# Rebuilding the opening of a hybrid attention layer: modulation sums on TensorE, rotation tables inside attention

## The chip, the cores and the metric

The kernel runs on one core of one Trainium2 chip. A core has five engines with an instruction stream each: TensorE (PE in the profile; its weight loads are PEld), VectorE (DVE), ScalarE (ACT), GpSimd (POOL) and SyncE (SP), which here issues nearly all transfers. An engine takes its instructions in the order in which they stand; engines wait for each other by semaphores. The metric is the device time of one execution in microseconds (us), as the median of several runs.

## The reference

One layer of an encoder: 1024 tokens of width 1024, all in float32. A conditioning vector `c` gives six vectors that shift, scale and gate; the change touches how the first two, shift and scale of the first norm, are computed.

```
mod = silu(c) @ w_ada + b_ada            # 6 x 1024
sh_a, sc_a, g_a, sh_m, sc_m, g_m = split(mod, 6)
h = rmsnorm(x, g_attn_norm) * (1 + sc_a) + sh_a
q_lat, kv_lat, k_rope, ca_qkv = split(h @ w_in)
q = rmsnorm(rmsnorm(q_lat) @ w_q_up)     # 8 heads of 64 + 32
k, v from rmsnorm(kv_lat) @ w_kv_up, k_rope
q, k = rope on the last 32 columns (positions up to some thousands)
o_mla = chunk-causal attention(q, k, v)  # 8 latent heads
o_ca = attention over a 9-chunk band with relative bias  # 8 band heads
x = x + g_a * (concat(o_mla, o_ca) @ w_out)
h = rmsnorm(x, g_mlp_norm) * (1 + sc_m) + sh_m
u = causal_depthwise_conv3(h @ w_up); gate, val = split(u)
x = x + g_m * ((silu(gate) * val) @ w_down)
```

## The kernel before

**Precision and stages.** Products keep float32 quality by splitting each operand into a high and a low part (`hi_of`, L77 to L80, and `lo_of`, L83) and adding three products (`gemm3`, L172 to L174). The kernel is one pass: an opening stage, attention with the other projections as filler, the output projection, the MLP. Its text is sorted by a list scheduler when the program is built: each instruction goes to its engine's list in an order that follows readiness and priority, and not just the text. `tc.issue_after(x)` adds an edge: what is written inside stands behind instruction `x`. `tc.high_priority` moves attention's own steps ahead of filler.

**Opening stage.** SP loads the packed parameters, the eight tiles of `x`, `c` spread over all partitions, then per column block `d` (128 columns, eight of them) two tiles of modulation weights of 512 KB (`load_ada`, L230, tag `wa`, five buffers) and the first query-key weights (`load_w`, L206, raw tiles in three buffers). Each `x` tile gets its sum of squares on ScalarE (L285), its power on GpSimd (L123, L124) and its factor on VectorE (L287). For block `d` VectorE computes shift and scale by two reductions over 1024 products (L389) and one product (L390) into `modT`; `mod_transpose` lets TensorE turn four blocks of `x` (L364), ScalarE applies scale and shift (L369, L370), GpSimd or VectorE make the low part; then 24 products per block add to the first query-key projection in four banks of PSUM (`qk0`).

**Rotation tables.** `rope_tables` reduces position times frequency to an angle in a chain of small VectorE steps on 128x128 elements (L302, L303, L308, L335, L338, L343, L345, L346), takes two Sins on ScalarE (L344, L347) and multiplies gains into two tables (L353). The latent group's `f_m` and `f_up` read these tables much later.

**Tables of ScalarE.** Silu, Sin, Ln and Exp are looked up in a set of functions that has to be loaded. The build puts a load in front of an activation whose function is not in the set loaded at that place of the list; `act.preload_act_table_set(name)` is a load of a set chosen by name. The kernel has one, behind the second Sin:

```
with tc.issue_after(last_trig[0].ins):
    act.preload_act_table_set("natural_log_exp_and_others")
```

**Attention.** 32 units follow each other: 16 of the band heads, 16 of the latent heads, two query halves per head. A unit runs `guard` (a row minimum per query, L796 to L812), `mrow` (L820, L821), then per key block `st` (scores L858, Exp L862, second Exp L866 or a copy on GpSimd, low part on VectorE L869) and two blocks later `val` (L884 to L886) into one accumulator of PSUM with one buffer. After a unit's last block, Ln and Exp form the reciprocal (L891, L892) and VectorE multiplies it in (L893). Filler generators, called by `pace` on a budget of estimated TensorE time, run the other projections: values `f_v`, query-key `f_qk`, latent `f_m`, `f_up`, and `f_oca`; their normalisations use `rsqrt_att`, an Ln and an Exp per call (L137, L138) between VectorE steps. `f_ada` (L515, L520) computes the other modulation vectors on the side. Before the first unit, filler is run up to a budget of `W_IN / 2`, half of the first value projection.

Of the kernel before, what the change touches and what calls it, by code (L numbers as in the profile page):

```python
# [23 lines left out]
P = 128  # L24
# [8 lines left out]
BIG16 = 60000.0  # L33
BSC = 256.0
# [30 lines left out]
def layer_kernel(ctx, tc, I, out):  # L65
# [78 lines left out]
    hw = right.__enter__()  # L144
    att_pg = tc.tile_pool(name="apg", bufs=1, side="left")
# [6 lines left out]
    ps = psA.__enter__()  # L152
    startp = tc.tile_pool(name="start", bufs=1, side="left")
# [37 lines left out]

    def load_w(name, src, ncol, he="a", ssw=None):
        tiles = []
        for k in range(ND):
            if ncol <= 256:
                w = hw.tile([P, 2, 256], F32R, name=f"{name}s{k}", tag="ws", bufs=16)
                hi, lo = w[:, 0, :ncol], w[:, 1, :ncol]
            else:
                wh = hw.tile([P, 512], F32R, name=f"{name}h{k}", tag="ws", bufs=16)
                wl = hw.tile([P, 512], F32R, name=f"{name}l{k}", tag="ws", bufs=16)  # L200
                hi, lo = wh[:, :ncol], wl[:, :ncol]
            for c0 in range(0, ncol, 256):
                c = slice(c0, min(c0 + 256, ncol))
                raw = hw.tile([P, 256], F32, name=f"{name}r{k}_{c0}", tag="wr", bufs=3)
                rw = raw[:, :c.stop - c0]
                sp.dma_start(rw, src[:, k, c])  # L206
                if ssw is not None:
                    junk = qtile(f"{name}j{k}")
                    act.activation(junk[:, :c.stop - c0], rw, AF.Square, accum_out=ssw[:, k:k + 1])
                hi_of(he, hi[:, c], rw)  # L210
                lo_of("p", lo[:, c], rw, hi[:, c])
            tiles.append((hi, lo))
        return tiles
# [7 lines left out]
    for t in range(NT):  # L221
        xt = pgtile([P, D], F32, f"x{t}") if t < 4 else st.tile([P, D], F32, name=f"x{t}", tag="x", bufs=4)
        sp.dma_start(xt[:], I["x"][t * P:(t + 1) * P, :])
        xs.append(xt)
# [7 lines left out]

    csb = st.tile([P, D], F32, name="csb")
# [47 lines left out]
    load_ada(0)  # L281
# [8 lines left out]
    last_trig = []  # L290

    def rope_tables():
        buf = [st.tile([P, 4, NT, 16], F32, name=f"rt{i}") for i in range(6)]
        cnt = [-1]

        def T():
            cnt[0] += 1
            return buf[cnt[0] // 4 % 6][:, cnt[0] % 4]

        def rnd(src, q):  # L300
            o = T()
            dve.tensor_scalar(o, src, q, MAGIC, op0=MUL, op1=ADD)  # L302
            dve.tensor_scalar(o, o, MAGIC, None, op0=SUB)  # L303
            return o

        def fma(n, c, b):
            o = T()
            dve.scalar_tensor_tensor(o, n, c, b, op0=MUL, op1=ADD)  # L308
            return o

        p1 = _grid(TWO_PI, 2.0 ** -9)
        p2 = _grid(TWO_PI - p1, 2.0 ** -21)
        p3 = TWO_PI - p1 - p2

        def reduce(src):
            n = rnd(src, 1.0 / TWO_PI)
            r = fma(n, -p1, src)
            r = fma(n, -p2, r)
            return fma(n, -p3, r)
# [6 lines left out]
        nh = rnd(ang, 2.0 ** -20)  # L326
        rem = fma(nh, -(2.0 ** 20), ang)
        nm = rnd(rem, 2.0 ** -8)
        lo = fma(nm, -(2.0 ** 8), rem)
        tot = reduce(lo)  # L330
        for n, w in ((nh, 2.0 ** 20), (nm, 2.0 ** 8)):
            c = w - round(w / TWO_PI) * TWO_PI
            c1 = _grid(c, 2.0 ** -9)
            x = T()
            dve.tensor_scalar(x, n, c1, None, op0=MUL)  # L335
            x = fma(n, c - c1, reduce(x))
            y = T()
            dve.tensor_tensor(y, tot, x, op=ADD)  # L338
            tot = y
        tot = reduce(tot)  # L340
        pi_s = 3.1415925
        sn, cn, cl, c2, cl2 = T(), T(), T(), T(), T()
        dve.tensor_scalar(cl, tot, pi_s, -pi_s, op0=MIN, op1=MAX)  # L343
        act.activation(sn, cl, AF.Sin)  # L344
        dve.tensor_scalar(c2, tot, math.pi / 2, None, op0=ADD)  # L345
        dve.tensor_scalar(cl2, reduce(c2), pi_s, -pi_s, op0=MIN, op1=MAX)  # L346
        last_trig.append(act.activation(cn, cl2, AF.Sin))  # L347

        for tab, c0 in ((tabq, C_RQ), (tabk, C_RK)):
            for half, trig in ((0, cn), (1, sn)):  # L350
                for j in range(2):
                    o = half * 32 + j * 16
                    dve.tensor_tensor(tab[:, :, o:o + 16], trig,  # L353
                                      pk[:, c0 + j * 16:c0 + j * 16 + 16].unsqueeze(1)
                                      .to_broadcast([P, NT, 16]), op=MUL)

    rope_tables()


    def mod_transpose(src, k, h, row, pspool, psum_tag, pb, hpool, tag, tmp, nbuf, heng, leng):  # L360

        pt = pspool.tile([P, 512], F32, name=f"ht_ps{row}_{k}_{h}", tag=psum_tag, bufs=pb)
        for j in range(4):
            pe.transpose(pt[:, j * P:(j + 1) * P], src(j), ident[:])  # L364
# [5 lines left out]
        act.activation(v[:], pt[:], AF.Identity, scale=a, bias=b)  # L370
# [7 lines left out]
    wqk = load_w("wq0_", I["w_qk"][0], 256)  # L378
    qk0s = ps.tile([P, 1024], F32, name="qk0_s", tag="S", bufs=1)
    qk0t = [ps.tile([P, 512], F32, name=f"qk0_{i}", tag="ST", bufs=2) for i in range(2)]  # L380
    qk0 = [qk0s[:, :512], qk0s[:, 512:], qk0t[0][:], qk0t[1][:]]
    for d in range(ND):
        if d + 1 < ND:
            load_ada(d + 1)

        tmp = cst.tile([P, 1], F32, name=f"adat{d}", tag="adat", bufs=2)
        for i, (init, o) in enumerate(((bsc[:, d:d + 1], tmp[:]), (pk[:, C_B + d:C_B + d + 1], modT[:, 1, d:d + 1]))):
            w = wada[2 * d + i]
            dve.tensor_tensor_reduce(w[:], w[:], csb[:], 1.0, init, MUL, ADD, accum_out=o)  # L389
        dve.tensor_tensor(modT[:, 0, d:d + 1], tmp[:], pk[:, C_GA + d:C_GA + d + 1], op=MUL)  # L390
# [10 lines left out]
    with tc.issue_after(last_trig[0].ins):  # L401
        act.preload_act_table_set("natural_log_exp_and_others")
# [67 lines left out]
    def v_tiles(pl, name, n):  # L470
        vs = [pl.tile([P, 4, 2, 3, 64], F16, name=f"{name}{i}") for i in range(n)]
        for v in vs:
            dve.memset(v[:, :, 0, 1], 1.0)
            dve.memset(v[:, :, 1, 1], 0.0)
        return vs
# [9 lines left out]
    def f_v(pp):  # L485
        ssw = cst.tile([P, ND], F32, name=f"ssw{pp}")
        w = load_w(f"wv{pp}_", I["w_v"][pp], 256, ssw=ssw)
# [20 lines left out]
    def f_ada():  # L508
        for m in (2, 3, 4):
            for n in range(4):  # L510
                acc = atile(f"aacc{m}_{n}")
                c0 = m * D + n * 256
                for k in range(ND):
                    w = atile(f"aw{m}_{n}_{k}")
                    sp.dma_start(w[:], I["w_ada"][k * P:(k + 1) * P, c0:c0 + 256])  # L515
                    if k == 0:
                        with tc.issue_after(last_lo["v"].ins):
                            dve.tensor_scalar(acc[:], w[:], cs[:, 0:1], None, op0=MUL)
                    else:
                        dve.scalar_tensor_tensor(acc[:], w[:], cs[:, k:k + 1], acc[:], op0=MUL, op1=ADD)  # L520
# [49 lines left out]
    def f_m():  # L570
        w = load_w("wm_", I["w_m"], NM)
# [42 lines left out]
    def f_up_steps(gr):  # L614
        if gr == 0:
            right.__exit__(None, None, None)
# [106 lines left out]
    ident_h = at.tile([P, P], F16, name="ident_h")  # L723
    dve.tensor_copy(ident_h[:], ident[:])
    ident_b = at.tile([P, P], F16, name="ident_b")
    dve.tensor_scalar(ident_b[:], ident[:], BSC, None, op0=MUL)
    mk_q = at.tile([P, P], F16, name="mk_q")
    mk_k = at.tile([P, P], F16, name="mk_k")
    for m_ in (mk_q, mk_k):
        pool.memset(m_[:], 0.0)  # L730
    pool.memset(mk_q[0:1, 0:64], BIG16)
    pool.memset(mk_q[32:33, 64:128], BIG16)
    pool.memset(mk_k[32:33, 0:64], BIG16)
    mz = at.tile([P, QK + 4], F16, name="mz")
    for x in kts:
        dve.memset(x[64:65, 1], 1.0)
    dve.memset(mz[:], 0.0)

# [26 lines left out]
    class Unit:  # L765
# [58 lines left out]
        def st(u, x):  # L824
# [7 lines left out]
            with tc.high_priority(offset=OFF_S):  # L832
# [29 lines left out]
                act.activation(p[:, :w], s[:, :w], AF.Exp, scale=ninv)  # L862
# [6 lines left out]
                dve.tensor_tensor(hl[:, 1, :w], p[:, :w], hl[:, 0, :w], op=SUB)  # L869
# [74 lines left out]
    fillers = [("v0", f_v(0)), ("qk1", f_qk(1)), ("qk2", f_qk(2)), ("v1", f_v(1)), ("qk3", f_qk(3)),  # L944
# [5 lines left out]
    ca_done = []  # L950
    ga_done = []
# [31 lines left out]
    knots = [(0.0, W_IN / 2), (14 * C_CA, W_A), (16 * C_CA + 6 * C_M, W_A + W_UP + O_EARLY * W_O),  # L983
# [19 lines left out]
    def value():  # L1003
# [3 lines left out]
        return u.val(x)  # L1007

    while spent[0] < W_IN / 2:
# [375 lines left out]
def _inputs(a):  # L1385
# [34 lines left out]
    wa_a = np.stack([wa[:, D:2 * D], wa[:, :D]], 1).reshape(D, 2, ND, P).transpose(2, 1, 3, 0)  # L1420
    d = {
# [31 lines left out]
```

## Time and profile before

| what | value |
|---|---|
| median of 3 runs | 1436.58 us (1432.51 to 1441.64) |
| profiled execution, its own time | 1435.16 us |
| its span, first to last instruction | 1433.2 us |
| mean granted TensorE clock | 0.960 |
| first softmax (L862) starts | 108.3 us |
| last unit's Ln (L891) starts | 684.4 us |
| MLP's first Silu (L1251) | 791.4 us |

A row of the table of stretches gives, for a stretch of the span, the busy time and the number of instructions of each engine, the granted TensorE clock (1.00 is full speed), the mean busy share of the DMA engines and the GB/s moved. A row of instruction groups gives line, engine, operation, output and input tiles, count, busy time and mean ns of one, then the idle time ahead of them with what ended it. A row of a line's or a tile's answer gives minimum, median and maximum of the duration in ns, and the first and last start in us. A row of the timeline gives start, duration, engine, line, operation and, in brackets, the idle time before it and the releaser.

### The profile page before, as it was taken

What the parts mean: (1) busy time and instruction counts of PE and PEld (TensorE: products, weight loads), DVE (VectorE), ACT (ScalarE), POOL (GpSimd) and SP (SyncE); (2) the same over time, 40 slices, a digit from 0 to 9 for tenths busy, and PEclk for the clock granted to TensorE, in tenths of its full rate; (3) what the DMA queues carried; (4) which work ended last, traced back from release to release, by engine and by line L of the source; (5) the groups of instructions that cost most, each with busy time, mean ns of one, the idle gap of its engine ahead of it and who ended that gap; (6) DMA issues with size and microseconds to landing.
All of it is one profiled execution on the core that took longest, in us unless ns stands there. A gap on an engine that the chain in (4) does not pass through costs nothing.

```text
span 1433.2 us, 20250 instructions
## 1 busy us (share of the span) xinstructions
PE 1286.3 (90%) x6952; PEld 868.0 (61%) x6952; DVE 1071.7 (75%) x1721; ACT 806.8 (56%) x1517; POOL 728.2 (51%) x776
## 2 busy tenths in 40 slices
PE   3869999988867889898897999999999988999998
PEld 3758878866544556555663444444444437888887
DVE  8865775666789887876467999988888876666554
ACT  5446675555766766665476566666666533333331
POOL 5643234342345362524350787666666626666664
PEclk9979999999978999999998999999999998999999
DMA  8321223221110033332813632222221005446542
GB/s 313 118 92 38 82 73 109 87 74 45 56 41 22 16 103 99 105 100 84 315 61 117 212 104 89 88 89 89 88 89 59 30 30 206 146 141 225 181 152 103
DMA packets 83458, 153.03 MB, mean 107 GB/s; under 512 B 8598, under 2 KB 44698, under 8 KB 83356
## 3 DMA queue, kind: packets, MB, share of 16 engines
q1 hardware_dynamic: 83356, 151.75, 31.5%
q8 instruction: 54, 0.88, 0.2%
q14 instruction: 48, 0.39, 0.1%
HBM read 122.88 MB, written 28.84 MB: 106 GB/s over the span
## 4 chain that ended last, share of the span: by engine, by line
PE 59%; DVE 19%; DMA 9%; ACT 5%; issue 4%; POOL 2%; SPq 0%; DVEq 0%; ACTq 0%; POOLq 0%
PE p L1127 7%; PE p L1126 7%; PE p L1128 7%; DMA aw<-w_ada 6%; PE dn L1368 6%; PE dn L1369 6%; PE dn L1370 5%; PE tm L858 2%; DVE adaw L389 2%; DVE aacc L520 2%; PE tc L858 2%; DVE mz L812 1%; DVE hlm L869 1%; PE ipq L172 1%; PE ipq L174 1%
## 5 line engine op out<-in xcount | busy, mean ns | idle before, releaser
L83 POOL TENSOR_TENSOR wds<-wd,wds 128x512 fp32r<-128x512 f32 x88 | 152.1, 1748 | 105.1 <-ACT wds L77 105.1
L1368 PE MATMUL dn<-wds,g 128*128 128x512 f32 x352 | 136.8, 395 | 9.1 <-ACT g L77 9.1
L77 ACT ACTIVATE wds<-wd 128x512 fp32r<-128x512 f32 x88 | 54.7, 623 | 153.1 <-PE dn L1370 148.3
L1369 PE MATMUL dn<-wds,g 128*128 128x512 f32 x352 | 137.1, 392 | 0.0
L1370 PE MATMUL dn<-wds,g 128*128 128x512 f32 x352 | 135.6, 390 | 0.0
L1355 DVE TENSOR_TENSOR wd<-wd,gmbc 128x1024 f32<-128x1024 f32 x44 | 72.6, 1654 | 83.6 <-DMA wd<-w_down 81.4
L869 DVE TENSOR_TENSOR hlm<-pm,hlm 128x512 f16<-128x512 f32 (+2 forms) x96 | 66.4, 703 | 28.7 <-ACT hlm L866 17.4
L1368 PEld LDWEIGHTS dn<-wds,g 128*128 128x128 f32 x352 | 67.0, 191 | 23.6 <-ACT g L77 9.6
L1207 ACT ACTIVATE u<-c,pk,wcv 128x1024 f32<-128x1024 f32 x44 | 52.2, 1233 | 51.1 <-DVE c L1247 43.9
L520 DVE SCALAR_TENSOR_TENSOR aacc<-aw,cs,aacc 128x256 f32<-128x256 f32 x84 | 44.3, 528 | 47.7 <-DMA aw<-w_ada 47.4
L83 DVE TENSOR_TENSOR g<-gr,g 128x512 fp32r<-128x512 f32 x44 | 72.8, 1656 | 6.9 <-ACT g L77 6.8
L858 PE MATMUL tm<-qt,kt 96*128 96x512 f16 (+7 forms) x288 | 71.0, 344 | 6.8 <-ACT qt L821 4.0
L1369 PEld LDWEIGHTS dn<-wds,g 128*128 128x128 f32 x352 | 66.6, 189 | 14.1
L1370 PEld LDWEIGHTS dn<-wds,g 128*128 128x128 f32 x352 | 66.5, 189 | 13.8
L1208 DVE SCALAR_TENSOR_TENSOR u<-c,wcv,u 128x1023 f32<-128x1023 f32 x44 | 56.0, 1307 | 24.4 <-ACT u L1207 24.4
L862 ACT ACTIVATE pc<-tc,sca 128x512 f32<-128x512 f32 (+3 forms) x96 | 50.2, 523 | 41.6 <-DVE hlc L869 22.4
L862 ACT ACTIVATE pm<-tm,scm 128x512 f32<-128x512 f32 (+1 forms) x96 | 55.0, 578 | 29.4 <-PE tm L858 20.7
L858 PEld LDWEIGHTS <-kt 128*128 128x128 f16 (+2 forms) x480 | 46.3, 101 | 39.7 <-issue 21.5
L869 DVE TENSOR_TENSOR hlc<-pc,hlc 128x512 f16<-128x512 f32 (+3 forms) x96 | 51.6, 543 | 16.1 <-ACT hlc L866 10.3
L77 ACT ACTIVATE wd<-wu 128x512 f16<-128x512 f32 x22 | 13.9, 630 | 85.6 <-DVE wu L1138 85.6
L79 POOL TENSOR_SCALAR hlm<-pm 128x384 f16<-128x384 f32 (+2 forms) x48 | 27.6, 574 | 65.9 <-ACT pm L862 45.8
L858 PE MATMUL tc<-qt,kt 128*128 128x512 f16 (+3 forms) x192 | 55.0, 313 | 6.2 <-ACT hlc L866 3.9
(459 smaller groups left out, 4490.0 us busy)
## 6 DMA issues: line engine op xcount, KB each, us to landing
wu<-w_up SPq DMA_DIRECT2D x44, 512.0 KB, 4.6
wd<-w_down SPq DMA_DIRECT2D x44, 512.0 KB, 3.5
aw<-w_ada SPq DMA_DIRECT2D x96, 128.0 KB, 2.1
g_d<-u SPq DMA_DIRECT2D x22, 512.0 KB, 2.6
gr<-g_d SPq DMA_DIRECT2D x44, 256.0 KB, 3.5
adaw<-w_ada_a SPq DMA_DIRECT2D x16, 512.0 KB, 4.3
x<-x SPq DMA_DIRECT2D x8, 512.0 KB, 8.6
wq_r<-w_qk SPq DMA_DIRECT2D x32, 128.0 KB, 2.4
```

The source lines that it names most:

```text
L83: return (pool if eng == "p" else dve).tensor_tensor(o, i, f32(hi), op=SUB)
L520: dve.scalar_tensor_tensor(acc[:], w[:], cs[:, k:k + 1], acc[:], op0=MUL, op1=ADD)
L858: last = pe.matmul(s[:, c0:c1], l, m, start=(y == 0), stop=(y == len(todo) - 1))
L862: act.activation(p[:, :w], s[:, :w], AF.Exp, scale=ninv)
L869: dve.tensor_tensor(hl[:, 1, :w], p[:, :w], hl[:, 0, :w], op=SUB)
L1126: pe.matmul(pt, sh, pg[:, 0], start=(k == 0), stop=False)
L1127: pe.matmul(pt, sh, pg[:, 1], start=False, stop=False)
L1128: pe.matmul(pt, sl, pg[:, 0], start=False, stop=(k == 3))
L1355: dve.tensor_tensor(raw[:], raw[:], gmbc[:], op=MUL)
L1368: pe.matmul(pts[t][n], sh, w[n][:, 0], start=(j == 0), stop=False)
L1369: pe.matmul(pts[t][n], sh, w[n][:, 1], start=False, stop=False)
L1370: pe.matmul(pts[t][n], sl, w[n][:, 0], start=False, stop=(j == NF - 1))
```

## The change

The opening is rebuilt. In the order of the text:

- Small constants of attention (`ident_h`, `ident_b`, `mk_q`, `mk_k`, `mz`) are made at the start; the memsets of value and key tiles go from VectorE to GpSimd.
- The loads of modulation blocks 0 and 1 stand behind the fourth and the eighth `x` tile, ahead of `c`; later blocks are asked for two blocks ahead instead of one.
- Blocks 0 to 2 (`NPE = 3`) get their sums from TensorE: 16 products per block of a 128x128 weight piece with one column of `silu(c)`, the weights transposed on the host for that, and two small VectorE steps. Blocks 3 to 7 stay as they were.
- `load_w` is cut into `load_wk` for one row block; the first query-key weights are loaded one block ahead in the loop, and the first value weights (`wv0`) inside the loop from block 2 on. Two later weight tiles' ScalarE copies are held behind instructions of attention.
- `rope_tables` becomes a generator in buffers of its own. Nine steps (`ROPE_0`) run in the opening; the others by `rope_step`, once per step of `f_ada`, and `f_m` runs what is left. The two Sins become one over 128x256.
- The hold of the named table load is dropped together with `last_trig`.
- The third query-key filler comes ahead of the second value filler, which waits for the fourth unit (`p0_done`). The budget before the first unit is `0.95 * W_IN`.

```diff
+NPE, ROPE_0 = 3, 9
+INIT = 0.95
...
+    def load_wk(name, src, k, ncol, he="a", ssw=None):
...
+            held = last_lo["hv"] if name == "wq1_" else last_lo["exp"] if name == "wq2_" else None
+            with tc.issue_after(held.ins) if held is not None else nullcontext():
+                hi_of(he, hi[:, c], rw)
+            lo_of("p", lo[:, c], rw, hi[:, c])
+        return hi, lo
+
     def load_w(name, src, ncol, he="a", ssw=None):
...
+        return [load_wk(name, src, k, ncol, he, ssw) for k in range(ND)]
...
+    for t in range(NT):
+        xt = pgtile([P, D], F32, f"x{t}") if t < 4 else st.tile([P, D], F32, name=f"x{t}", tag="x", bufs=4)
+        sp.dma_start(xt[:], I["x"][t * P:(t + 1) * P, :])
+        xs.append(xt)
+        if t % 4 == 3:
+            load_ada(t // 4)
...
-    last_trig = []
...
-        act.activation(sn, cl, AF.Sin)
...
-        last_trig.append(act.activation(cn, cl2, AF.Sin))
...
+        act.activation(tr[:], tr[:], AF.Sin)
...
-    rope_tables()
+    rope = rope_tables()
+    for _ in range(ROPE_0):
+        next(rope)
+
+    def rope_step():
+        with tc.issue_after(last_lo["hl"].ins):
+            return next(rope, None)
...
+            with tc.issue_after(last_lo["pm"].ins) if k + h + j == 0 else nullcontext():
+                pe.transpose(pt[:, j * P:(j + 1) * P], src(j), ident[:])
...
+    wqk.append(load_wk("wq0_", I["w_qk"][0], 0, 256))
     for d in range(ND):
         if d + 1 < ND:
-            load_ada(d + 1)
...
+            wqk.append(load_wk("wq0_", I["w_qk"][0], d + 1, 256))
+        if d + 2 < ND:
+            load_ada(d + 2)
+        if d >= 2:
+            for k in range(*((0, 1, 2, 4, 6, 8)[d - 2:d])) if d < 7 else ():
+                wv0.append(load_wk("wv0_", I["w_v"][0], k, 256, ssw=ssw0))
+        if d < NPE:
+            pm = ps.tile([P, 512], F32, name=f"ada_ps{d}", tag="mm", bufs=2)
+            for i in range(2):
+                for k in range(ND):
+                    last_lo["pm"] = pe.matmul(pm[:, i:i + 1], wada[2 * d + i][:, k * P:(k + 1) * P], cs[:, k:k + 1],
+                              start=(k == 0), stop=(k == ND - 1))
+            dve.scalar_tensor_tensor(modT[:, 0, d:d + 1], pm[:, 0:1], bsc[:, d:d + 1], pk[:, C_GA + d:C_GA + d + 1],
+                                     op0=ADD, op1=MUL)
+            dve.tensor_tensor(modT[:, 1, d:d + 1], pm[:, 1:2], pk[:, C_B + d:C_B + d + 1], op=ADD)
+        else:
...
     startp.__exit__(None, None, None)
-    with tc.issue_after(last_trig[0].ins):
-        act.preload_act_table_set("natural_log_exp_and_others")
+    act.preload_act_table_set("natural_log_exp_and_others")
...
-            dve.memset(v[:, :, 0, 1], 1.0)
-            dve.memset(v[:, :, 1, 1], 0.0)
+            pool.memset(v[:, :, 0, 1], 1.0)
+            pool.memset(v[:, :, 1, 1], 0.0)
...
-                        with tc.issue_after(last_lo["v"].ins):
+                        with tc.issue_after(last_lo["hl"].ins):
...
-    fillers = [("v0", f_v(0)), ("qk1", f_qk(1)), ("qk2", f_qk(2)), ("v1", f_v(1)), ("qk3", f_qk(3)),
+    fillers = [("v0", f_v(0)), ("qk1", f_qk(1)), ("qk2", f_qk(2)), ("qk3", f_qk(3)), ("v1", f_v(1)),
...
-            if key == "oca" and not ca_done:
+            if key == "oca" and not ca_done or key == "v1" and not p0_done:
...
                     next(side[0], None)
+                    rope_step()
...
-    while spent[0] < W_IN / 2:
+    while spent[0] < INIT * W_IN:
         fill_step()
...
+    wa_a[:NPE] = np.stack([wa[:, D:D + NPE * P], wa[:, :NPE * P]]).reshape(2, ND, P, NPE, P).transpose(3, 0, 2, 1, 4).reshape(NPE, 2, P, D)
```

`rsqrt_att`, unchanged, is called by the fillers and by the first head's normalisation:

```
act.activation(t, ss, AF.Ln)
act.activation(rr, t, AF.Exp, scale=-0.5)
```

More of the change, by code (lines that the diff above doesn't have):

```diff
@@ L144, in layer_kernel @@
     hw = right.__enter__()
+    ropep = tc.tile_pool(name="rope", bufs=1, side="right")
+    rp = ropep.__enter__()
     att_pg = tc.tile_pool(name="apg", bufs=1, side="left")
@@ L287, in layer_kernel @@
         dve.tensor_scalar(xt[:], xt[:], rx[:, t:t + 1], None, op0=MUL)
-    last_trig = []
     def rope_tables():
-        buf = [st.tile([P, 4, NT, 16], F32, name=f"rt{i}") for i in range(6)]
+        buf = [rp.tile([P, 4, NT, 16], F32, name=f"rt{i}") for i in range(5)]
         cnt = [-1]
@@ L722, in layer_kernel @@
     qts = [at.tile([P, 2, 512], F16, name=f"qt{i}") for i in range(NQ)]
[L723 to L734, printed above, removed]
     for x in kts:
-        dve.memset(x[64:65, 1], 1.0)
-    dve.memset(mz[:], 0.0)
+        pool.memset(x[64:65, 1], 1.0)
     def turned(src, rows, nm):
@@ L1006, in value @@
             need(u.needv)
[L1007 to L1009 removed]
+        c = u.val(x)
+        if u.n == 3 and x == len(u.blocks) - 1:
+            p0_done.append(1)
+        return c
+    while spent[0] < INIT * W_IN:
         fill_step()
```

123 lines of the change are left out of this document (71 added, 52 removed).

## The prediction

> **What bounds the kernel now.** I read the page's totals first, then the table of stretches, cut where the work changes, then single rows. The stretches are the stage of first projections (to 62 us), its tail until the first softmax (108.3), the band heads (to 393.7), the mixed part in which the latent group is projected (to 508.5) and the rest of attention.
>
> ```profile
> span 1433.2 us, 20250 instructions
> PE 1286.3 (90%) x6952; PEld 868.0 (61%) x6952; DVE 1071.7 (75%) x1721; ACT 806.8 (56%) x1517; POOL 728.2 (51%) x776
> ...
> core 0: us, PE busy (x) PEld busy (x) DVE busy (x) ACT busy (x) POOL busy (x), PEclk, DMA share, GB/s
> 0.00:40.00 40.00, 17.51 (x89) 14.09 (x90) 35.70 (x122) 22.09 (x37) 24.44 (x38) 1.00 0.89 311
> 40.00:62.00 22.00, 16.91 (x120) 15.54 (x119) 21.79 (x29) 9.98 (x17) 17.61 (x13) 0.92 0.41 131
> 62.00:89.50 27.50, 13.89 (x80) 12.31 (x79) 21.10 (x56) 14.91 (x45) 12.38 (x22) 0.64 0.24 77
> 89.50:108.30 18.80, 18.80 (x143) 17.78 (x140) 6.33 (x22) 5.88 (x16) 7.61 (x11) 0.89 0.23 71
> 108.30:393.70 285.40, 261.25 (x1947) 217.94 (x1946) 194.70 (x487) 180.20 (x437) 98.12 (x182) 0.98 0.24 71
> 393.70:508.50 114.80, 88.87 (x483) 57.83 (x482) 103.08 (x278) 81.99 (x196) 53.26 (x102) 0.88 0.10 27
> 508.50:684.40 175.90, 152.50 (x854) 94.66 (x851) 127.16 (x227) 104.48 (x190) 75.50 (x83) 0.96 0.31 101
> ```
>
> The reader is to see three limits. To 62 us it is VectorE (35.70 of 40, then 21.79 of 22). In the band heads TensorE is busy 92% of the time. From 393.7 VectorE leads again (103.08 of 114.8, 90%), and TensorE drops to 77%: 90% is the most that a crowded engine other than TensorE reaches here, and I use it as ceiling. ScalarE has room everywhere: 63%, 71% and 59% in the last three stretches. The whole change is aimed at the first stage; the last three stretches, 576 us, decide what its side effect costs.
>
> ```profile
> L108 ACT ACT_TABLE_LOAD x1 | 1.3, 1283 | 0.7 <-PEq L1438 0.7
> L402 ACT ACT_TABLE_LOAD x1 | 1.3, 1283 | 0.0
> L1251 ACT ACT_TABLE_LOAD x1 | 1.3, 1283 | 0.0
> ...
> 27.20 0.31 ACT L347 ACTIVATE rt<-rt 128x128 f32<-128x128 f32 x1
> 27.53 1.28 ACT L402 ACT_TABLE_LOAD   x1
> 29.18 0.78 ACT L369 ACTIVATE hT<-ht_ps,modT 128x512 fp32r<-128x512 f32 x1 [0.37 <-DVE modT L389]
> ```
>
> Three table loads of 1283 ns are all that ScalarE does of that kind. The one at 27.53, requested by name and held behind the second Sin, brings a set with both Ln and Exp; nothing reloads until the MLP.
>
> **The side effect: ScalarE's tables.** The change drops the hold, and the named load has no other operand to wait for. In the program as built it comes out as ScalarE's first instruction, ahead of the load for the first Silu, which replaces it. From then on each Ln and each Exp that follows the other gets a load of its own, because the build takes for each a set that lacks the other; and the Sin, now inside attention, would have displaced the shared set anyway. ScalarE's list begins its first normalisation like this:
>
> ```
> L139 LoadActFuncSet
> L139 Activation rt<-ss
> L140 LoadActFuncSet
> L140 Activation r<-rt
> ```
>
> I count 134 loads in the list, against 3: two at the start, six before the first softmax, 66 over the instructions that fill the band stretch of before, 34 in the mixed one, 25 in the rest of attention, one for the MLP. Each takes 1.283 us of ScalarE in order, so behind it stand whatever exps and evictions follow. Stage by stage:
>
> Band heads: 180.2 + 66 x 1.283 = 264.9 of 285.4 us, 93%. Seven evictions of the first values leave it, at 0.468 us (row below), 3 us. TensorE is at 92% here, so two engines would be nearly full, each with waits on the other. If ScalarE never waits, there is no growth; at the 90% ceiling 262 needs 291, +6; with every load exposed it is +85. I take +18, near the ceiling's end, since most loads stand before an instruction whose input is awaited anyway.
>
> Mixed part: 82.0 + 34 x 1.283 = 125.6 us of ScalarE in 114.8. This cannot fit. At full use it is +11, at the 90% ceiling 139.6, +25, with all exposed +44. I take +25.
>
> Rest of attention: 104.5 + 25 x 1.283 = 136.6 of 175.9, so room is there, but each head's end has a chain:
>
> ```profile
> 572.05 0.22 PE L886 MATMUL pvm<-hlm,vm 128*128 128x128 f16 x1
> 572.31 0.59 ACT L891 ACTIVATE rim<-pvm 64x512 f32<-64x512 f32 x1 [0.90 <-PE pvm L886]
> 572.93 0.63 ACT L892 ACTIVATE rim<-rim 64x512 f32<-64x512 f32 x1
> 574.56 0.76 DVE L893 SCALAR_TENSOR_TENSOR rim<-pvm,vabm,rim 64x512 f32<-64x512 f32 x1
> 575.37 0.38 PE L884 MATMUL pvm<-hlm,vm 128*128 128x512 f16 x1 [0.18 <-DVE rim L893]
> ```
>
> Ln, Exp and a multiply read the head's only accumulator, and the next head's first product waits for the multiply. The load ahead of Ln fits into the 0.90 us idle at least in part; the one ahead of Exp is in the chain. Twelve head ends at 0 to 2 x 1.283 us give 0 to +31; the shown wait of TensorE is only 0.18 us and other work stands between, so I take half of one load each, +8.
>
> On the size of one load the Trainium skill, ScalarE: Activation LUTs, section "What ACT_TABLE_LOAD costs", gives 1283 ns and about 1380 ns more of draining. The load itself agrees; the drain does not show at 27.53, where the next activation starts 0.37 us after the load's end. By the page's 2.66 us the 125 loads in attention would be 333 us of ScalarE instead of 160, far over its room.
>
> **The opening stage.**
>
> ```profile
> L389 DVE CUSTOM_DVE_ANT_0 adaw<-adaw,csb,bsc x8: 1273/1668/1749, 20.9 to 56.2; 128x1024 f32<-128x1024 f32 x8
> L389 DVE CUSTOM_DVE_ANT_0 adaw<-adaw,csb,pk x8: 1271/1734/2367, 23.8 to 58.5; 128x1024 f32<-128x1024 f32 x8
> ...
> DMA to landing us min/median/max: 2.6/4.3/10.2
> ...
> L308 DVE SCALAR_TENSOR_TENSOR rt<-rt 128x128 f32<-128x128 f32 x13 | 4.1, 321 | 0.0
> L353 DVE TENSOR_TENSOR tabq<-rt,pk 128x128 f32<-128x128 f32 x4 | 1.4, 383 | 0.0
> L473 DVE MEMSET vca<- 128x256 f16 x6 | 1.6, 272 | 0.0
> ...
> L174 PE MATMUL qk<-wq_s,hT x32: 277/282/418, 33.2 to 70.8; 128*128 128x256 f32 x32
> ...
> L481 ACT ACTIVATE vca<-ipv,vabc 128x256 f16<-128x256 f32 x15 | 7.0, 468 | 14.2 <-PE ipv L174 7.6 <-DVE vca L483 6.4
> ...
> 25.20 0.78 ACT L369 ACTIVATE hT<-ht_ps,modT 128x512 fp32r<-128x512 f32 x1 [3.47 <-DVE modT L390]
> 89.28 0.27 PE L796 MATMUL sc<-kt,qt 128*128 128x128 f16 x1 [2.47 <-DVE kt L912]
> ...
> L535 PE MATMUL p_ada<-ones,aacc x32: 164/250/271, 242.6 to 666.0; 128*128 128x1 f32 x32
> ...
> L172 PE MATMUL ipq<-wq_s,hT x192: 277/283/472, 119.6 to 284.3; 128*128 128x256 f32 x192
> ```
>
> VectorE loses six of the sixteen reductions, 6 x 1.7 = 10.2 us, some fifteen steps of the angle chain at 0.32 and eight table products at up to 0.38 (together 7.8), and memsets such as the six at 0.27 (1.6). The moved steps go to the band stretch, where VectorE is busy 68%: nothing, or +8 without that cover. The memsets go to GpSimd, 34% busy there: nothing, or +2. TensorE gains 48 one-column products; the nearest row has 0.25 us each, 12 us, in a stretch where it is busy 17.51 of 40: nothing, or +12. Two blocks of modulation weights (2 MB) pass x and c on SP's queue: at 311 GB/s the last four x tiles come 3.2 us later, unseen, since block 0's sums are what the first product of before waits for (25 us). Eight value tiles (1 MB, 3.4 us of transfers) and their splits move to before 62 us.
>
> What is late next: block 2's two buffers stay occupied until its products are done, and in TensorE's list those stand between the query-key products of blocks 0 and 1. So three of five buffers turn over for blocks 3 to 7, at (4.3 + 1.67) / 3 = 2.0 us a reduction. Some 8.1 MB stand ahead of block 3, landed by about 30 us at 311 GB/s with the start. In VectorE's list block 2's scale and shift come behind the first reduction of block 6, the seventh: 30 + 6 x 2.0 + 1.7 = 44 us. SP's queue stands still with that. TensorE cannot go past block 2's transposes; before, it had followed VectorE block by block. It then owes 6 x 32 instructions for blocks 2 to 7, 192 for the first values and some 70 for the first head, at 0.131 us each (18.80 / 143): 60 us, to 104. Before reaches that state at 119.6, where the next projection starts. So -16 without any stall. The chain of normalisation gives another end: query-key products end near 44 + 252 x 0.131 = 77; before ended them at 70.8 and had its first score at 89.28, 18.5 us on; the six loads add 7.7, so 103. From that score to the state at 119.6 before needs 30 us, 12 of them for value products that are done by then, and 8 us of the next projection are done early: 113, so -6. If TensorE does its 60 us at the clock of 0.64 seen from 62 to 89.5 instead of 0.89, it ends at 44 + 83 = 127, +8. I take -6, as that chain ends later than TensorE's work at the usual clock. The swap of the third query-key and second value projections, and the wait of the latter for the fourth head, reorder filler of equal cost: nothing, or a few us if the filler runs dry.
>
> Sum: -6 + 18 + 25 + 8 = +45. The profiled execution took 1435.16 us (span 1433.2 and 2.0 around it), 1.4 under the median of 1436.58; 1435 + 45 = 1480.
>
> **Rivals.** (1) Faster: the loads run in ScalarE's idle time. It is idle 576 - 367 = 209 us in attention, and 160 us of loads is less. Then only the opening counts, -16, 1419. Against it: the mixed part does not fit, +11 at least. It decides if the band stretch runs with ScalarE above 93%. (2) A balance: opening -14, mixed part +15, a few us elsewhere: 1435 to 1449. For it: a load that stands before an awaited input costs nothing. (3) Loads mostly exposed, because two full engines wait on each other: half to all of +85, +44 and +31 give +80 to +160, 1515 to 1595. For it: TensorE's 77% beside a 90% VectorE. (4) ScalarE also empties at each load. The gap after L402 is 0.37; the only room in a row for more would be a wait that a profile puts down to something else. Priced at one load's length again (2.57 us): band 180 + 170, mixed 82 + 87, rest 104 + 64; at 90% ceilings 389, 188 and 187, which is +104, +73 and +11, less 6: 1617. This is what the skill's page named above states. (5) The change does not shorten the opening at all, by block 2's wait: +8 there, 1494; it lies in my range.
>
> **How the numbers follow.** Chances: the forecast with its bounds, (5) among them, 1450 to 1530, 0.70; (1) 0.08; (2) 0.12; (3) beyond 1530 0.07; (4) 0.03. A measurement here tells about 1% from no change (the three runs spread 0.6%), that is 1422 to 1451. Faster 0.08, same 0.13, slower 0.79. The range 1440 to 1535 leaves out (1), a third of (2) and the far part of (3) and (4).
>
> **What would show it.** ACT_TABLE_LOAD rows by the hundred at the lines of Ln and Exp; ScalarE near 975 us busy; ScalarE above 85% in the band and mixed parts; block 2's first transposed tile near 44 us; the second query-key projection starting between 105 and 130. I am wrong if the table loads number a few, if the stretch that held 393.7 to 508.5 is not longer, or if the opening alone is over 20 us shorter.

## The result, and the profile after

| | before | after |
|---|---|---|
| median, 4 runs each on one chip | 1435.98 us | 1535.63 us |
| ratio, 95% interval | | 1.069 [1.066, 1.073] |
| profiled execution's span | 1433.2 us | 1534.3 us |
| table loads on ScalarE | 3 | 134 |

The change makes the kernel 100 us slower. First the page of after: its span, the busy time of each engine with the share of the span, and the chain that ended last, shared out by engine.

```profile
span 1534.3 us, 20548 instructions
...
PE 1332.6 (87%) x7048; PEld 901.0 (59%) x7048; DVE 1042.2 (68%) x1680; ACT 973.9 (63%) x1647; POOL 729.3 (48%) x808
...
PE 57%; ACT 18%; DVE 11%; issue 6%; DMA 6%; POOL 2%; SPq 0%; ACTq 0%; DVEq 0%; POOLq 0%
```

The same chain in the page of before:

```profile
PE 59%; DVE 19%; DMA 9%; ACT 5%; issue 4%; POOL 2%; SPq 0%; DVEq 0%; ACTq 0%; POOLq 0%
```

ScalarE went from 5% of the chain to 18%: 276 us instead of 72. Its share of busy time rose much less, from 56% to 63%. Whoever reads only busy shares sees an engine with a third of its time free.

The table of stretches of after, cut at the same events as that of before (to 62 us, first softmax at 106.0, the Ln of the fourteenth of the 16 band units at 434.3, that of the fourth of the 16 latent units at 585.3, last unit's Ln at 784.2). Columns: stretch, its length, busy time and instructions of PE, PEld, DVE, ACT, POOL, then granted clock, DMA share, GB/s. The cut that the prediction calls the end of the band heads is that fourteenth Ln; in both kernels the last two band units end inside the mixed part.

```profile
0.00:40.00 40.00, 26.71 (x154) 26.74 (x155) 25.87 (x98) 21.65 (x41) 23.43 (x43) 1.00 0.89 317
40.00:62.00 22.00, 19.56 (x147) 18.50 (x147) 16.16 (x31) 14.27 (x31) 17.08 (x19) 0.93 0.43 156
62.00:106.00 44.00, 38.89 (x309) 37.58 (x308) 21.21 (x51) 25.63 (x49) 21.49 (x39) 0.96 0.14 43
106.00:434.30 328.30, 272.81 (x1873) 218.77 (x1871) 202.13 (x509) 263.87 (x504) 103.40 (x200) 0.91 0.22 65
434.30:585.30 151.00, 98.30 (x471) 62.94 (x471) 98.31 (x268) 124.74 (x226) 52.62 (x102) 0.74 0.07 20
585.30:784.20 198.90, 160.80 (x850) 99.86 (x848) 118.74 (x222) 135.10 (x214) 72.42 (x83) 0.89 0.28 89
784.20:1534.00 749.80, 715.57 (x3252) 436.64 (x3252) 559.82 (x504) 388.65 (x586) 438.85 (x327) 0.98 0.36 124
```

The opening is a little shorter (first softmax 2.3 us earlier) and the part from 784 us on is as long as before (749.8 against 748.8). Nearly all that was lost lies between: 328.3, 151.0 and 198.9 us where before had 285.4, 114.8 and 175.9. In these stretches TensorE, which led the band heads at 92%, is down to 83%, 65% and 81%, and its granted clock in the mixed part is 0.74 instead of 0.88. VectorE, at 90% of the mixed part before, is at 65%. ScalarE is at 80%, 83% and 68%. So no engine is full, and still all three take longer.

The table loads in the groups of instructions (count, busy us and mean ns of one, idle time ahead):

```profile
L139 ACT ACT_TABLE_LOAD x34 | 43.6, 1283 | 0.6
L931 ACT ACT_TABLE_LOAD x31 | 39.8, 1283 | 1.9 <-DMA oT_d<-rim 1.4
L140 ACT ACT_TABLE_LOAD x27 | 34.6, 1283 | 0.5
L932 ACT ACT_TABLE_LOAD x21 | 26.9, 1283 | 0.4
```

The rest stand mostly at the softmax's Exp (L901, 15). L139 and L140 are the Ln and Exp of a normalisation, L931 and L932 those of a head's end. The count is the forecast one, and so is the length.

What such a load does is seen in the timeline of after in the mixed part (start, us, engine, line, operation, tiles; in brackets the idle time before and its releaser):

```profile
481.52 1.28 ACT L139 ACT_TABLE_LOAD   x1
481.56 0.48 PE L897 MATMUL tc<-qt,kt 128*128 128x384 f16 x1 [3.26 <-ACT hlc L905]
...
482.82 0.21 ACT L139 ACTIVATE rtu<-uss 128x8 f32<-128x8 f32 x1
483.04 1.28 ACT L901 ACT_TABLE_LOAD   x1
484.34 0.69 ACT L901 ACTIVATE pc<-tc,sca 128x512 f32<-128x512 f32 x1
...
485.07 0.48 PE L897 MATMUL tc<-qt,kt 128*128 128x384 f16 x1 [2.19 <-ACT pc L901]
```

ScalarE has no gap here; it is full for 3.5 us. But 2.56 us of that are two loads for one Ln of 0.21 us: one load changes to the Ln's set, the next one changes back for the softmax. The softmax's Exp of `pc` stands behind both. TensorE's next scores wait for that Exp, which reads the old ones, and TensorE idles 2.19 us. The stretch as a whole gives no hint of this: ScalarE's idle time lies elsewhere, and it does not help the `pc` that waits now.

At a head's end the second load is in the chain itself:

```profile
651.66 1.28 ACT L931 ACT_TABLE_LOAD   x1
652.95 0.59 ACT L931 ACTIVATE rim<-pvm 64x512 f32<-64x512 f32 x1
...
654.27 1.28 ACT L932 ACT_TABLE_LOAD   x1
655.56 0.63 ACT L932 ACTIVATE rim<-rim 64x512 f32<-64x512 f32 x1
...
656.22 0.76 DVE L933 SCALAR_TENSOR_TENSOR rim<-pvm,vabm,rim 64x512 f32<-64x512 f32 x1 [0.19 <-ACT rim L932]
```

From the start of Ln to the multiply that frees the accumulator are 3.27 us; the head's end shown of before took 2.25.

### The profile page after: what moved, and what is told of

Same layout as the page of the kernel before. It is cut to its first block, busy times and chain, and to the rows that moved or that the text cites. A ratio compares the mean times of both kernels' runs of the same rounds, so it can differ in the third digit from the quotient of the medians.

```text
span 1534.3 us, 20548 instructions
## 1 busy us (share of the span) xinstructions
PE 1332.6 (87%) x7048; PEld 901.0 (59%) x7048; DVE 1042.2 (68%) x1680; ACT 973.9 (63%) x1647; POOL 729.3 (48%) x808
## 4 chain that ended last, share of the span: by engine, by line
PE 57%; ACT 18%; DVE 11%; issue 6%; DMA 6%; POOL 2%; SPq 0%; ACTq 0%; DVEq 0%; POOLq 0%
PE p L1171 7%; PE p L1172 7%; PE p L1173 7%; PE dn L1413 5%; PE dn L1414 5%; PE dn L1415 5%; PE tm L897 3%; DMA aw<-w_ada 3%; ACT L931 2%; ACT L139 2%; ACT L140 1%; PE tc L897 1%; ACT L932 1%; ACT pc L901 1%; DVE mz L851 1%
## 5 line engine op out<-in xcount | busy, mean ns | idle before, releaser
L897 PE MATMUL tm<-qt,kt 96*128 96x512 f16 (+7 forms) x288 | 76.7, 361 | 18.5 <-ACT hlm L905 8.3
L897 PE MATMUL tc<-qt,kt 128*128 128x512 f16 (+3 forms) x192 | 58.7, 333 | 34.0 <-ACT hlc L905 22.5
L908 DVE TENSOR_TENSOR hlm<-pm,hlm 128x512 f16<-128x512 f32 (+2 forms) x96 | 61.6, 648 | 30.0 <-ACT hlm L905 16.4
L1413 PEld LDWEIGHTS dn<-wds,g 128*128 128x128 f32 x352 | 67.0, 191 | 23.7 <-ACT g L79 9.6
L897 PEld LDWEIGHTS <-kt 128*128 128x128 f16 (+2 forms) x480 | 49.6, 107 | 47.5 <-issue 28.7
L901 ACT ACTIVATE pm<-tm,scm 128x512 f32<-128x512 f32 (+1 forms) x96 | 55.0, 578 | 24.7 <-PE tm L897 13.0
L901 ACT ACTIVATE pc<-tc,sca 128x512 f32<-128x512 f32 (+3 forms) x96 | 50.1, 524 | 24.8 <-DVE hlc L908 14.2
```

The lines of the kernel that those rows point to most:

```text
L897: last = pe.matmul(s[:, c0:c1], l, m, start=(y == 0), stop=(y == len(todo) - 1))
L901: last_lo.setdefault("exp", act.activation(p[:, :w], s[:, :w], AF.Exp, scale=ninv))
L908: lo = dve.tensor_tensor(hl[:, 1, :w], p[:, :w], hl[:, 0, :w], op=SUB)
L1413: pe.matmul(pts[t][n], sh, w[n][:, 0], start=(j == 0), stop=False)
```

## The experiments

**Theories.** A: the loads cost the time. A1, of the prediction: they cost it because ScalarE runs out of room. A2: they cost it because ScalarE takes its list in order, so that a load makes late what stands behind it, however much room ScalarE has elsewhere. Rivals: the loads are mostly hidden, and the remade order of the work or the rebuilt opening costs the time. All kernels compute the whole layer.

**1. After, with the set loaded by name at the right place.**

```diff
-        act.activation(tr[:], tr[:], AF.Sin)
+        sin = act.activation(tr[:], tr[:], AF.Sin)
+        with tc.issue_after(sin.ins):
+            act.preload_act_table_set("natural_log_exp_and_others")
```

> The changed kernel with one more named load of the Ln-and-Exp set, held behind the Sin; every engine's list is otherwise the same, and ScalarE's table loads fall from 134 to 15. Theory A (the loads cost the time, about 0.9 us each after the 14 us that the opening gained): 1535 - 119 x 0.9 = 1428, between 1415 and 1440. Rival B (the moved rotation steps, memsets and the filler order cost it): above 1510. Rival C (the loads cost the 51 us of the prediction's three stages, and something else the rest): near 1485.

Apart from the loads (15 instead of 134) each engine's list is that of after, instruction by instruction. Measured: 1432.27 us, ratio to before 0.995 [0.993, 0.996]. So 119 loads cost 102 us by the spans of the two profiles (1534.3 - 1432.4), or 107 by the two ratios: 0.86 to 0.90 us each. Theory A had 1428, between 1415 and 1440. Everything else that the change did is still there, and that kernel is no slower than before. The rivals fall. The three stretches of attention of this kernel, in the same columns:

```profile
108.20:395.60 287.40, 260.88 (x1870) 214.30 (x1867) 198.44 (x499) 186.78 (x445) 104.42 (x199) 0.94 0.26 73
395.60:504.10 108.50, 85.38 (x470) 55.59 (x470) 97.88 (x271) 80.55 (x191) 50.85 (x99) 0.91 0.10 28
504.10:682.80 178.70, 156.38 (x852) 97.65 (x852) 121.21 (x229) 104.56 (x191) 73.93 (x84) 0.92 0.31 98
```

Against it after has +40.9, +42.5 and +20.2 us, for 60, 34 and 24 loads: experiment 1 keeps six in the band heads and none behind them. That is 0.68, 1.25 and 0.84 us a load. Some 70% of the first two is idle time of TensorE (55.5 - 26.5 = 29 and 52.7 - 23.1 = 29.6 us); the rest is the same number of products running slower. Where TensorE waits is in its waits over attention (line, releaser, us in total, times, longest us). After:

```profile
PE tc L897 <- ACT hlc L905: 22.5, 12, 4.2
PE qu L189 <- ACT uqr L704: 14.1, 3, 6.4
PE sm L835 <- DVE mz L851: 14.0, 11, 4.5
...
PE tc L897 <- ACT pc L901: 11.4, 9, 3.1
PE pvm L924 <- DVE rim L933: 10.9, 6, 3.6
```

And with the set named (its line numbers are two higher):

```profile
PE sm L837 <- DVE mz L853: 7.8, 11, 1.1
...
PE qu L189 <- ACT uqr L706: 5.4, 3, 2.5
PE tc L899 <- ACT hlc L907: 4.5, 6, 1.1
...
PE tc L899 <- ACT pc L903: 0.7, 2, 0.6
```

What grew most is the wait of scores (`tc`) for the two Exps that read the old ones (`pc`, `hlc`), and that of the latent projection (`qu`) for a normalised input. The row minima (`sm`) behind VectorE and the value products (`pvm`) behind the multiply at a head's end (1.2 us with the set named) wait longer too.

**2. Before, with nothing but the hold dropped.**

```diff
-    with tc.issue_after(last_trig[0].ins):
-        act.preload_act_table_set("natural_log_exp_and_others")
+    act.preload_act_table_set("natural_log_exp_and_others")
```

> The kernel before, only its named load no longer held behind the Sin, so that ScalarE's list has 141 loads instead of 3. Theory A: 1436 + 138 x 0.9 = 1560, between 1535 and 1580. Rival B: within 10 us of 1436. Rival C: near 1490.

Measured: 141 loads, 1548.93 us, ratio 1.076 [1.074, 1.077], within theory A's bounds. Apart from a few neighbouring instructions that change places, each engine's list is that of before. One edge dropped in a kernel with the old opening costs 109 us, 0.79 per load. The loss of after does not need the rest of the change.

**3. Room or order.** With `HI_ON = "pp"` the high part of every softmax block is a copy by GpSimd; with `"pa"` ScalarE makes every second one by another Exp. It is put on top of after, and on top of experiment 1; the two kernels' lists are the same but for the loads (142 and 15).

```diff
-HI_ON, HL_BUFS = "pa", 3
+HI_ON, HL_BUFS = "pp", 3
```

> The changed kernel with every second Exp replaced by a copy on GpSimd, which takes some 55 us (48 at 0.52 and 48 at 0.60) off ScalarE in attention; 142 loads. Read against the run beside it, which has the same lists on all engines and 15 loads. Theory A1 (the loads cost what ScalarE has no room for): the pair is about 50 us apart instead of 105. Theory A2 (the loads cost because they stand in chains that TensorE waits for, or stop the exps behind them): 127 x 0.87 = 110 apart, within 15.

> The run with 15 loads and every second Exp replaced by a copy on GpSimd. Against the run with 15 loads alone: GpSimd becomes slower per block, so 1432 to 1460. The pair's distance is what tells A1 (50) from A2 (110).

Measured: 1549.21 us, ratio 1.077 [1.073, 1.080], with the loads; 1438.45 us, ratio 1.000 [0.997, 1.002], with 15. The two are 111 us apart, where A2 had 110 and A1 50. First the band heads and the mixed part with 142 loads, then with 15:

```profile
106.90:440.00 333.10, 274.18 (x1877) 221.03 (x1875) 211.22 (x512) 252.14 (x468) 128.03 (x248) 0.91 0.22 64
440.00:590.20 150.20, 101.29 (x471) 63.66 (x471) 97.01 (x261) 117.83 (x207) 61.26 (x112) 0.76 0.07 19
```

```profile
108.00:397.30 289.30, 260.50 (x1873) 215.18 (x1872) 208.18 (x510) 170.88 (x403) 128.93 (x243) 0.94 0.26 73
397.30:504.70 107.40, 85.76 (x474) 54.68 (x474) 97.03 (x260) 72.15 (x172) 63.95 (x116) 0.92 0.10 27
```

ScalarE has 16 us more room in the band heads and 8 more in the mixed part than in experiment 1 (170.88 and 72.15 against 186.78 and 80.55). Had room been the limit, the loads would cost that much less. They cost +43.8 and +42.8, where they cost +40.9 and +42.5 in experiment 1. Per load, of 64 and 36 here, that is 0.68 and 1.19 us, against 0.68 and 1.25. A1 falls, A2 stands.

**4. The named load only at the first latent head.** After, with the load behind that head's first Exp:

```diff
-                last_lo.setdefault("exp", act.activation(p[:, :w], s[:, :w], AF.Exp, scale=ninv))
+                pexp = act.activation(p[:, :w], s[:, :w], AF.Exp, scale=ninv)
+                last_lo.setdefault("exp", pexp)
+                if not u.band and "named" not in last_lo:
+                    last_lo["named"] = pexp
+                    with tc.issue_after(pexp.ins):
+                        act.preload_act_table_set("natural_log_exp_and_others")
```

> The changed kernel with a named load behind the first latent head's first Exp, so that the 80-odd loads ahead of it stay and those behind it go: 95 loads. If each stage pays for its own loads, the band and mixed parts keep their cost and the rest gets back its share: 1535 less 20 to 45, so 1490 to 1515. If the late stages only inherit the delay of the band, 1530.

Measured: 95 loads, 1499.13 us, ratio 1.040 [1.036, 1.044]. The band heads keep their 66 loads and take 329.3 us (after: 328.4). The first latent head starts inside the mixed part, which keeps 20 of its 34 loads, against the expectation that it keeps its cost: it falls from 151.0 to 132.2 us, still 23.7 over experiment 1. The rest has no load left and falls from 198.9 to 181.7, 3.0 over experiment 1. Each stage pays for its own loads, and nothing is made up later.

**5. Loads added to before.** Two redundant loads of the set that is in place at each of the 32 head ends: one behind the unit's last Exp, one behind its Ln.

```diff
+                    extra_load(u.last_exp)
-                    act.activation(ri[r0], u.pv[r1], AF.Ln)
+                    ln = act.activation(ri[r0], u.pv[r1], AF.Ln)
+                    extra_load(ln)
```

Here `extra_load(x)` is the named load inside `tc.issue_after(x.ins)`.

> The kernel before with two more named loads at each of the 32 head ends, one behind the last Exp ahead of Ln and one between Ln and Exp: 64 loads more, 82 us of ScalarE, of a set that is loaded already, so that nothing else changes but the order that the scheduler finds. If every load in attention costs the 0.8 to 0.9 us of the runs so far, 1440 + 54 = 1494. If loads at head ends are cheap, since the first of a pair fits ahead of the wait and the chain has room, 1440 + 10 to 25. If they are the dear ones, near 1440 + 82.

Measured: 1478.31 us, ratio 1.025 [1.022, 1.028]: 39 us for 64 loads, 0.61 each, between the expected 10 to 25 and 54. Unlike the build's own loads, these are seen by the scheduler, which made the lists anew around them. By stage it is +15.5 for 28 loads, +14.6 for 12 and +12.2 for 24. The mixed part again takes nearly the whole length of each load: 1.22 us here, 1.25 in after, 1.19 in experiments 3 and 4, and 0.99 in experiment 2. In the band heads a load costs 0.55 here, all at head ends, and 0.68 to 0.72 in after and experiments 2 and 3, where about half stand in normalisations. So the stage seems to count for more than the instruction that a load precedes; why is not tested.

**6. The opening, with the tables right.** After, with the first named load held behind the Silu of `c` and a second one behind the Sin (5 loads in all):

```diff
-    act.activation(csb[:], csb[:], AF.Silu)
+    silu = act.activation(csb[:], csb[:], AF.Silu)
...
+        with tc.issue_after(sin.ins):
+            act.preload_act_table_set("natural_log_exp_and_others")
...
-    act.preload_act_table_set("natural_log_exp_and_others")
+    with tc.issue_after(silu.ins):
+        act.preload_act_table_set("natural_log_exp_and_others")
```

> The changed kernel with the first named load held behind the second Silu and another behind the Sin: 5 loads. Theory A: ten loads fewer than in the run with 15, some of them ahead of the first softmax: 1420, between 1408 and 1435. Rival B: above 1505. Rival C: near 1480.

Measured: 1426.44 us, ratio 0.990 [0.989, 0.992], within theory A's bounds. This beats both kernels, by 13 us and by 109. The four experiments below each take one part of the change out of this kernel. In each the scheduler also gave the engines other orders, in attention too, so a difference is that of the edit together with the order that came of it.

| kernel | median us | ratio, 95% | first softmax | fourteenth band unit's Ln | mixed part's end | last unit's Ln |
|---|---|---|---|---|---|---|
| tables right | 1426.44 | 0.990 [0.989, 0.992] | 106.2 | 392.3 | 502.9 | 680.5 |
| rotation in the opening | 1425.42 | 0.989 [0.987, 0.992] | 102.4 | 387.1 | 500.4 | 676.0 |
| sums by VectorE | 1436.20 | 0.997 [0.995, 0.999] | 103.9 | 389.0 | 505.1 | 689.4 |
| old load order | 1441.78 | 1.001 [1.000, 1.003] | 115.2 | 402.4 | 518.9 | 693.0 |
| half the filler | 1441.22 | 1.001 [1.000, 1.003] | 100.5 | 395.7 | 511.2 | 690.6 |

All rotation steps in the opening, with one named load behind Silu and Sin (3 loads):

```diff
-    for _ in range(ROPE_0):
-        next(rope)
+    for _ in rope:
+        pass
```

> As the run with 5 loads, but all steps of the rotation tables back in the opening, with one named load behind the Sin: 3 loads. If the moved steps were worth something, the opening gets up to 8 us longer (the steps' busy time on VectorE): 1420 to 1430. If VectorE is not what the opening waits for any more, the same as the run with 5 loads within 4 us, or 2 to 3 us faster for two loads fewer.

The interval covers that of the kernel above, and the first softmax comes 3.8 us earlier, not later: stepping the tables in attention is worth nothing that these runs can tell. In after VectorE is busy for 16.16 of the 22 us from 40 to 62, where before had 21.79, so there is room for them.

All modulation sums by VectorE's reductions:

```diff
-NPE, ROPE_0 = 3, 9
+NPE, ROPE_0 = 0, 9
```

> The run with 5 loads, with all eight blocks' sums back on VectorE's reductions (no products on TensorE). If the products on TensorE are what shortens the opening: 6 x 1.7 = 10 us more, 1434 to 1440. If the order of the loads and the earlier value weights do it: 1424 to 1430.

The 10 us came out near the expectation, but for another reason than it gave. The first query-key product starts 3.6 us later (37.8 for 34.1), but the first softmax is 2.3 us earlier; the loss lies in the mixed part (116.1 us instead of 110.6) and behind it (184.4 instead of 177.6), far from the edit. That the products on TensorE shorten the opening is not shown.

Blocks 0 and 1 loaded after `x` and `c`, as before:

```diff
         xs.append(xt)
-        if t % 4 == 3:
-            load_ada(t // 4)
...
+    load_ada(0)
+    load_ada(1)
```

> The run with 5 loads, with the modulation blocks 0 and 1 loaded behind all of x and c as before. If the new order of the loads is worth its place: the first product on TensorE starts some 3 to 5 us later and the end 3 to 5 us later, 1430 to 1432. If block 2's release or the transfers set the pace: 1426 within 3.

A miss: 15 us instead of 3 to 5. The first product does start 3.3 us later, as expected, but the query-key products end at 86.0 us instead of 75.4. Nine of the 15 us are in the opening. The stretch up to the first softmax in the kernel with the tables right:

```profile
62.00:106.20 44.20, 40.21 (x323) 39.09 (x322) 21.07 (x55) 18.52 (x44) 22.72 (x42) 0.96 0.15 44
```

and with the old load order:

```profile
62.00:115.20 53.20, 49.40 (x401) 48.27 (x400) 23.83 (x59) 23.60 (x52) 26.39 (x45) 0.97 0.12 36
```

TensorE is busy for over 90% of both, so this stretch is as long as its work, and with the late loads it has 78 instructions more to do from 62 us on.

Half of the first value projection before the first unit, as before:

```diff
-INIT = 0.95
+INIT = 0.5
```

> The run with 5 loads, with the filler ahead of the first head back at half of the first value projection. If the value products that run ahead of the first head fill TensorE's idle time, giving them back costs up to 12 us (96 products at 0.131): 1430 to 1438. If they only change places: 1426 within 3.

A miss as well: 15 us later, where 4 to 12 or nothing had been expected. The first softmax comes 5.8 us earlier, and the band heads end 3.4 us later: they take 295.2 us instead of 286.1. The early start is given back, and more, within the next stage. Each of the two, old order and half filler, loses the whole gain of 13 us by itself, so the parts' worths do not add up. How much of either loss is the new order of the work is open.

## Why the prediction was right or wrong

**The mechanism and the sign: right.** The loads by the hundred, 1283 ns each, ScalarE busy 973.9 us for a forecast 975, their number by stage (66, 34 and 24 in the three stretches of attention for 66, 34 and 25). Experiment 2 shows that the dropped hold alone does it.

**The opening's -6: near in size, by luck as to its place.** Experiment 1 is the change with most of its loads gone; as in the sum, six stand ahead of the first softmax. Its ratio puts the whole kernel at -8 us (-5 to -10). The start of the forecast chain held. Block 2's first transposed tile came at 44 us, behind the late scale of `modT`:

```profile
44.12 0.78 ACT L402 ACTIVATE hT<-ht_ps,modT 128x512 fp32r<-128x512 f32 x1 [4.54 <-DVE modT L439]
```

The query-key products ended at 74.7 us for a forecast 77. Then the chain parts from the runs: the first score came at 96.2 us for 103, and the second query-key projection started ahead of the first softmax and of the 105 to 130 forecast, where before had it behind the softmax (119.6):

```profile
L189 PE MATMUL ipq<-wq_s,hT x192: 277/283/562, 99.2 to 250.5; 128*128 128x256 f32 x192
```

The forecast's 0.131 us per instruction came from a stretch with a granted clock of 0.89; between 62 and 106 us it was 0.96. In the profiles of experiment 1 and of before the first softmax starts at the same time (108.2 and 108.3), the next stretch is 2.0 us longer and the rest of attention 2.8; only the mixed part is shorter, by 6.3. These two executions lie 0.8 us apart, so they do not place the 8 us either. That the opening gained them is not shown.

**The size of the three load terms: wrong, by half.** Forecast +18, +25 and +8, measured +41, +42.5 and +20. The failed step is the price of a load as the prediction put it: "near the ceiling's end, since most loads stand before an instruction whose input is awaited anyway", with growth only where ScalarE passes 90%, and at a head's end "half of one load each". With every load exposed the prediction had +85, +44 and +31; the runs show 48%, 97% and 65% of that, where 21%, 57% and 26% were taken (the first is for 60 loads instead of 66, and 53% of their length).

Experiment 1 shows that the premise was false, since its list holds the same activations without the loads. If their inputs were awaited, ScalarE would stand idle before them. In its mixed part (count, busy us and mean ns of one, idle time ahead):

```profile
L140 ACT ACTIVATE ur<-rtu 128x8 f32<-128x8 f32 x14 | 2.9, 207 | 0.3
L139 ACT ACTIVATE rtu<-uss 128x8 f32<-128x8 f32 x14 | 2.9, 207 | 3.4 <-DVE uss L134 3.3
```

Over all of attention 118 activations have a load in after and none in experiment 1. There 98 of them follow the activation before within 0.1 us, and the idle time before all 118 is 22 us (3 of it in the mixed part), where the loads are 151 us long. There was little waiting in which a load could hide.

The ceiling failed too. ScalarE never reached it (80%, 83%, 68%; above 85% had been forecast for the first two), experiment 3 shows that more room changes nothing, and the 90% came from one stretch: in the same table VectorE is at 99% from 40 to 62 us. What a load meets is not an average share but the exps and evictions behind it, which TensorE waits for. That the mixed part passes on nearly the full length because the latent projections, a normalisation each, and the scores depend on each other within a few us is an argument from the timeline, and no run tests it.

**Part of the size is TensorE's own.** The same 26 products in the mixed part (count, busy us and mean ns of one), in after and with the set named:

```profile
L191 PE MATMUL qu<-wq,latT 128*128 128x384 f32 x26 | 10.7, 412 | 0.0
```

```profile
L191 PE MATMUL qu<-wq,latT 128*128 128x384 f32 x26 | 9.8, 376 | 0.0
```

TensorE's busy time there is 98.3 us against 85.4 for the same list, at a granted clock of 0.74 against 0.91: 13 of the 42.5 us come as slower products, which no term of the sum had. In the band heads it is 12 of the 40.9.

**The rivals.** (1) and (2) rested on ScalarE's idle time, and fell with A1. (4), an emptying of ScalarE at each load, is excluded: of the 131 loads from the first normalisation to the last head's end in after, 130 start within 0.03 us of the end of the activation before, and in 128 the next activation starts within 0.14 us of the load's end. The Trainium skill (ScalarE: Activation LUTs, section "What ACT_TABLE_LOAD costs") has some 1380 ns of draining beside the load; in this kernel it does not show. (5), an opening that takes 8 us longer at a clock of 0.64, did not come: from 62 us to the first softmax the clock was 0.96. (3), loads mostly exposed, is what happened, and with two engines that wait on each other as it said; but they were not full.

## What to carry to other kernels

A table load by name needs an edge behind the last activation of another set; without an operand or an edge it came first in the list here, and the next Silu undid it, so count the table loads in the built list after each change. A stall put into an engine that works in order, with others waiting for what stands behind it, cost 53% to 97% of its length here, in stages where that engine was at most 83% busy: ask who waits for the instructions behind it, and whether the engine was idle just there, and not how much of it is idle over the stage. The rest of the change is worth 1% once the two edges are in place.

## What was not expected of the hardware

TensorE's granted clock fell where TensorE waited more: 0.74 against 0.91 in the mixed part with the same products, 0.91 against 0.94 and 0.89 against 0.92 beside it. In after's mixed part the longest waits of TensorE are 6.4, 5.3 and 4.5 us; with the set named none is over 2.5. The Trainium skill (TensorE: Matmul & The Clock Gate, Part 1) says that the array drops to half rate after an idle window of about 3.4 us. The long waits of after agree with that, and by it a wait of over 3.4 us would cost more than itself. The 0.91 does not follow from single waits of that length, since there are none: the trace has the clock at half for three times 6.8 us there, and in the 3.4 us ahead of each TensorE was busy for 28%, 53% and 51%. No run here separates the clock from the waits.
